# Last-value rows loaded before the first keys, and value differences formed from the fifth pair on with three buffers

## The chip, the cores and the metric

The kernel runs on one core of a Trainium2 chip. A core has five engines with queues of their own: TensorE (PE in the profile, with PEld for its weight loads), VectorE (DVE), ScalarE (ACT), GpSimd (POOL) and SyncE (SP). In this kernel SP issues nearly all DMAs; its queue is in order, and so is each other engine's. The metric is the device time of one execution in microseconds, lower is better.

## The reference

One step of a hybrid encoder layer, for a prompt of 1024 tokens and 64 new tokens of a running stream with 512 cached ones. Cut to what matters:

```python
def project(x, norm_w, w_in, q_norm_w, k_norm_w):
    h = rms_norm(x, norm_w) @ w_in                      # 1024 -> 6144 columns
    sb_q, sb_k, sb_v, sb_z, cb_q, cb_k, cb_v, cb_z, g_sb, g_cb = jnp.split(h, SPLIT_POINTS, axis=-1)
    ...                                                 # cb_q and cb_k are normalized per head

def stick_breaking(q, k, v, q_pos, k_pos):
    z = jnp.einsum("bqhd,bkhd->bhqk", q, k).astype(jnp.float32) * ATTN_SCALE
    causal = k_pos[None, :] < q_pos[:, None]
    log_beta = jax.nn.log_sigmoid(z)
    log_keep = jnp.where(causal, jax.nn.log_sigmoid(-z), 0.0)
    suffix = lax.cumsum(log_keep, axis=3, reverse=True) - log_keep
    w = jnp.where(causal, jnp.exp(log_beta + suffix), 0.0)
    return jnp.einsum("bhqk,bkhd->bqhd", w.astype(v.dtype), v)

def merge(x, o_sb, z_sb, o_cb, z_cb, g_sb, g_cb, w_proj_sb, w_proj_cb, w_out):
    b_sb = (o_sb * jax.nn.silu(z_sb)) @ w_proj_sb
    b_cb = (o_cb * jax.nn.silu(z_cb)) @ w_proj_cb
    h = jax.nn.sigmoid(g_sb) * b_sb + jax.nn.sigmoid(g_cb) * b_cb
    return x + h @ w_out
```

The second branch (cb) is a softmax attention over a band of nine chunks of 64 keys. There are eight heads of 64 in each branch. Projected keys and values are also outputs.

## The kernel before

**Stages.** The first stage (to 226 us) normalizes and transposes x and forms the projections whose tokens stay on the partitions: the values of both branches and the queries and keys of cb. The second stage (226 to 531 us) forms the rest of the input projection in 14 *pairs* of 128-column units: pairs 1 to 4 are keys and queries of sb, 5 to 8 the gates z, 9 to 12 the sigmoid of the sb gate, 13 and 14 part of the cb gate. Each pair runs seven steps `s` of 2 x 12 matmuls (L672), one product of a fast 2 x 2 scheme, so there are 98 steps, counted by `n`. The third stage is attention: stick-breaking (sb) over 4 pairs of heads and then the band (cb), with the four last projection units as fill work between (L832). Then come the merge and the output projection.

**Differences of values.** The stick-breaking weights of a query row are differences of a running product, so the kernel multiplies the running products with differences of values instead: row t of `d_dv` in DRAM is value row t-1 minus value row t, and the last value of each query tile is added afterwards (`vl`, L1181). The 26 jobs of 128 rows (L628 to L634) are spread over the second stage. `dv_load` (L610) loads two tiles, `dva` with the rows shifted by one (L614 where there is no row before the first: 127 rows, the first being zeroed by POOL; L618 else) and `dvb` with the rows themselves (L620). `dv_sub` (L623) subtracts on POOL (L625) and puts the store to `d_dv` (L626) on the list that `step()` empties at the next step. `dv_step` loads at odd n and subtracts at even n, as soon as two jobs are loaded. Both tiles have two buffers.

**Around it.** Each pair's results go through `emit` (L567): ACT writes them into an `hl` tile (L574 for gates, L580 for keys and queries; four buffers), DVE completes it (L576, L581), and the store to DRAM (L571, L51) is issued by SP at the next step. Weights of the next pairs are loaded by SP too (L391), split by ACT, DVE and POOL (L435, L436, L403). All of these stand in the order in which the code is written; there is no scheduler.

**Between the stages.** After the pairs, SP loads what the first scores need: keys of the cache and of the new tokens (`kss`), queries of the new tokens (`sqs`), keys (`ks`) and queries of the prompt (`sq`, of which three tiles cover query tiles 0 to 2, 3 to 5 and 6, 7), then the differences (`vp`, `vs`) and the gate (`zt`). Between these loads stand six calls of `fill(24)`, each of which gives PE 24 fill matmuls, and the stores of their results (`d_gcb<-sg`, L745). `load_vl` (L723) loads the last value row of every query tile, 8 + 1 rows, into `vrow`; `make_vl` (L727) transposes them on PE after the six fills and before the first scores (L1080). The scans of `imp` and `ims` (L715, L719) on DVE prepare two masks in the same pool of buffers as `vrow`.

**DMA slots.** SP's DMAs count on eight semaphores in turn (DMAHW0 to DMAHW7), and a DMA waits until the one eight places before it has landed. An engine that takes over memory of the earlier stage waits for all the eight.

Of the kernel before, what the change touches and what calls it, by code (L numbers as in the profile page):

```python
# [8 lines left out]
F32 = mybir.dt.float32  # L9
# [23 lines left out]
def hybrid_step_kernel(ctx: ExitStack, tc: tile.TileContext, x_prompt, x_sample, c_sbk, c_sbv, c_cbk, c_cbv,  # L33
# [26 lines left out]
    def xc(t):  # L60

        return t * 128 if t < 4 else HF + (t - 4) * 128
# [69 lines left out]
    def load_unit(j):  # L132
        c = units[j][1]
        W.load(("u", j), wpool, w_in[:, c:c + 128].rearrange("(k p) n -> p k n", p=128), [128, KT, 128])
# [7 lines left out]
    def xk(s, k):  # L142
        return xhl[s][k // 4][:, k % 4]
# [56 lines left out]
    with ExitStack() as ph:  # L200
# [192 lines left out]
        def presum(n):  # L393

            i, s = divmod(n, 7)
            if i >= len(pairs) or s not in (1, 4, 6):
                return
            a, b = slice(0, 128), slice(128, 256)
            r1, r2 = raws[2 * i], raws[2 * i + 1]

            def total(x, y, op):
                d = ws.tile([128, 4, 128], F32, name="ws")
                V.tensor_tensor(out=d, in0=x, in1=y, op=op)  # L403
                return d[:]

            if s == 1:
                sums[1] = total(r1[:, :, b], r2[:, :, b], OP.add)
                sums[2] = total(sums[1], r1[:, :, a], OP.subtract)
            elif s == 4:
                sums[3] = total(r1[:, :, a], r1[:, :, b], OP.subtract)  # L410
                load_raw(2 * i + 3)
            else:
                sums[4] = total(r2[:, :, a], sums[2], OP.subtract)

        def prep(n):

            i, s = divmod(n, 7)
            if i >= len(pairs):
                return
            a, b = slice(0, 128), slice(128, 256)  # L420
            r1, r2 = raws[2 * i], raws[2 * i + 1] if s else None
            if s == 0:
                src = r1[:, :, a]
            elif s == 3:
                src = r2[:, :, a]
            elif s == 5:
                src = r2[:, :, b]
            else:
                src = sums[{1: 2, 2: 1, 4: 3, 6: 4}[s]]
            shape = [128, 2, 4, 128]  # L430
            if s in (2, 3, 4):
                t = natx.tile(shape, F32R, name="wlox" if s == 3 else "whix", bufs=2)
            else:
                t = wpool.tile(shape, F32R, name="whi" if s in (0, 5) else "wlo", bufs=2)
            A.activation(t[:, 0], src, AF.Copy)  # L435
            G.tensor_tensor(out=t[:, 1], in0=src, in1=t[:, 0].bitcast(F32), op=OP.subtract)  # L436
            blk[n] = t
            if s == 6:
                load_raw(2 * i + 4)
# [12 lines left out]
        for i in range(nb):  # L452
            for ti, t in enumerate(TO):
# [7 lines left out]
                for m, (k, n) in enumerate(steps):  # L461
# [3 lines left out]
                    x = xs[:, k] if t == 8 else xk(n % 2, k)[:, xc(t):xc(t) + r]  # L465
# [80 lines left out]
    with ExitStack() as ph:  # L546
        up = ph.enter_context(tc.tile_pool(name="a2u", bufs=3, side="right"))
# [7 lines left out]
        def step():  # L555
            for e in later[:]:
                e[0] -= 1
                if e[0] < 0:
                    later.remove(e)
                    e[1]()  # L560
# [47 lines left out]
        dvs = []  # L608

        def dv_load(r0, rows_, cur, prev, c):  # L610
            a, b = (up.tile([128, 256], F32, name=x, bufs=2) for x in ("dva", "dvb"))
            if len(prev) == 1 and prev[0] is None:
                G.memset(a[0:1], 0.0)
                SP.dma_start(a[1:rows_], cur[0:rows_ - 1, c])  # L614
            else:
                o = 0
                for q in prev:
                    SP.dma_start(a[o:o + q.shape[0]], q[:, c])  # L618
                    o += q.shape[0]
            SP.dma_start(b[:rows_], cur[:, c])  # L620
            dvs.append((r0, rows_, c, a, b))
# [29 lines left out]
        for i in range(len(pairs)):  # L651
            bank, s1, u2, u3 = {}, {}, {}, {}
            for s in range(7):
                n = 7 * i + s
                prep(n + LEAD)
                presum(n + LEAD + 1)
                if n + LEAD == 7 * len(pairs) + 2:
                    W.split(("u", 0))
                if n + LEAD == 7 * len(pairs) + 1:
                    load_unit(1)  # L660
                step()
                if i > 1:
                    dv_step(n % 2)
                w = blk.pop(n)
                for c, (a, b) in enumerate(XC):
                    m = b - a
                    if s < 3:
                        bank[BANK[s], c] = psB.tile([128, 512], F32, name=f"b{BANK[s]}{c}")
                    ps = bank[BANK[s], c]
                    for k in range(4):  # L670
                        for e, (hl_, x) in enumerate(((0, 0), (0, 1), (1, 0))):
                            TE.matmul(ps[:, :m], w[:, hl_, k], right[s](x)[:, k, a:b], start=s < 3 and k == 0 and e == 0,  # L672
                                      stop=k == 3 and e == 2, skip_group_check=s > 2)
                    if s == 0:
                        s1[c] = up.tile([128, 288], F32, name="s1")
                        A.activation(s1[c][:, :m], ps[:, :m], AF.Copy)
                    elif s in (1, 4):
                        u = up.tile([128, 288], F32, name="u2" if s == 1 else "u3")
                        (u2 if s == 1 else u3)[c] = u
                        V.tensor_tensor(out=u[:, :m], in0=ps[:, :m], in1=s1[c][:, :m], op=OP.add)  # L680
                    elif s == 3:
                        emit(i, 0, 0, c, ps, True)
                    elif s == 5:
                        V.tensor_tensor(out=s1[c][:, :m], in0=ps[:, :m], in1=s1[c][:, :m], op=OP.add)  # L684
                        emit(i, 1, 0, c, s1[c], False)
                    elif s == 6:
                        V.tensor_tensor(out=u2[c][:, :m], in0=ps[:, :m], in1=u2[c][:, :m], op=OP.add)
                        emit(i, 0, 1, c, u2[c], False)
                if s == 4:
                    for c, (a, b) in enumerate(XC):  # L690
                        m = b - a
                        V.tensor_tensor(out=u3[c][:, :m], in0=bank["3", c][:, :m], in1=u3[c][:, :m], op=OP.add)
                        emit(i, 1, 1, c, u3[c], False)
# [29 lines left out]
    def load_vl():  # L723
        SP.dma_start(vrow[0:8], d_sbv[0:NP].rearrange("(t q) c -> t q c", q=128)[:, 127])
        SP.dma_start(vrow[8:9], d_sbv[T - 1:T])
# [54 lines left out]
    def load_v(b, p):  # L780
        src, cache, n0 = (d_dv, d_dv[NP:NP + PAST], NP + PAST) if b == "sb" else (d_cbv, c_cbv, NP)
        c = slice(p * 128, (p + 1) * 128)
        vp = am.tile([128, 8, 128], F32, name="vp", bufs=2)
        vs = am.tile([128, 5, 128], F32, name="vs", bufs=1)
        SP.dma_start(vp, src[0:NP, c].rearrange("(t q) c -> q t c", q=128))
        SP.dma_start(vs[:, 0:4], cache[:, c].rearrange("(t q) c -> q t c", q=128))
        SP.dma_start(vs[0:64, 4], src[n0:n0 + NS, c])
        VP[b, p] = (vp, vs)
# [7 lines left out]
    def load_k(b, p, s):  # L796
        if s:
            place_k(alloc_k((b, p), 1), d_cT[b][p][:], 0, 512, 0, 512)
            place_k(KS[(b, p), 1], d_kT[b][p][:], NP, T, 512, 576)
        else:  # L800
            place_k(alloc_k((b, p), 0), d_kT[b][p][:], 0, NP, 0, NP)
# [345 lines left out]
    def load_z(b, p, j):  # L1147
        zt = am.tile([128, 256], F32, name="zt", bufs=4)
        nq = 256 if j < 4 else 64
        SP.dma_start(zt[:, :nq], d_z[b][p][:, 256 * j:256 * j + nq])  # L1150
        zts[b, p, j] = zt
# [59 lines left out]
    def load_bias(h):  # L1211
# [6 lines left out]
        if h % 2:  # L1218
            bs = BI["s", h // 2] = ab.tile([128, 576], F32, name="bsm", bufs=1)
            for w in range(2):  # L1220
                src = d_rb[h - 1 + w][0:1, 127:128]
                SP.dma_start(bs[64 * w:64 * w + 64], bass.AP(tensor=src.tensor, offset=src.offset,
                                                             ap=[[767, 64], [1, 576]]))

    load_k("sb", 0, 1)
    for f in (lambda: load_q("sb", 0, 3), lambda: load_k("sb", 0, 0), lambda: load_q("sb", 0, 0),
              lambda: (load_v("sb", 0), load_z("sb", 0, 4)), load_vl, lambda: None):
        fill(24)
        flush()
        f()  # L1230
# [10 lines left out]
    for i in range(len(seq) + LAG + 1):  # L1241
        m = 0
        if i < len(seq):
            b, p, t, hd = seq[i]
# [30 lines left out]
        if 0 <= i - LAG < len(seq):  # L1275
            tr(i - LAG)
            b, p, t, hd = seq[i - LAG]
# [182 lines left out]
    for i in range(2):  # L1460
# [3 lines left out]
        for q, s in enumerate(OP_):  # L1464
# [14 lines left out]
            for c in range(2) if s != "b" else ():  # L1479
# [25 lines left out]
                if s in (3, 4, 5, 6):  # L1505
# [3 lines left out]
                    x = {3: xrs.pop((i, w, half, c)) if s == 3 else None, 4: None, 5: s1[c], 6: u2[c]}[s]  # L1509
                    if s == 4:  # L1510
                        p, x = u3[c], xrs.pop((i, 1, 1, c))
# [61 lines left out]
```

## Time and profile before

| what | us |
|---|---|
| runs shown | 1003.59, 1005.52, 1006.38; median 1005.52 |
| profiled execution | 1004.52, its span 1002.7 |
| PE busy | 964.6, granted clock 0.993 on the mean |
| second stage (14 pairs) | 226 to 531 |
| fills before attention | 531 to 554.8 |
| first transposes of `vrow` | 560.31 |

All times in rows are counted from the span's start. A row of waits reads "engine line <- what ended the wait: total us, times, longest us"; one of a timeline "start us, length us, engine line operation out<-in xcount", with the idle time ahead of it and what ended that in brackets. SPq and ACTq are the engines' own queues, where DMAs are issued and semaphores awaited.

### The profile page before, as it was taken

Reading aid. Unit: us, or ns where it says so; the run is one execution under the profiler, and the core shown is the slowest. Engines: PE = TensorE matmul, PEld = TensorE weight load, DVE = VectorE, ACT = ScalarE, POOL = GpSimd, SP = SyncE. Lnnn points to the kernel's source line nnn. Section 1 sums busy time; section 2 is a strip of 40 time slices with the busy share of each in tenths; the row PEclk is TensorE's granted clock in tenths of the full one; section 3 lists DMA queues with packets and bytes.
Section 4 is the critical chain, followed back from the end, with each engine's and each line's share of the span. In section 5 each row is a group of like instructions: output and inputs, shape, how many; then the busy total and the mean of one; then the engine's idle time right before and its main releaser. Section 6 shows DMA issues by size and latency. Waiting matters only on the chain.

```text
span 1002.7 us, 20526 instructions
## 1 busy us (share of the span) xinstructions
PE 964.6 (96%) x7620; PEld 918.0 (92%) x7620; DVE 592.6 (59%) x1168; ACT 479.5 (48%) x1056; POOL 360.8 (36%) x325
## 2 busy tenths in 40 slices
PE   5999999999999899999999799999999899999998
PEld 5999999999999899999999688877978787999998
DVE  5456673894454465533222369776667666499745
ACT  5544443444443333334332367666877776465320
POOL 3276663205454566565430000000210100386551
PEclk9999999999999999999999799999999999999999
DMA  7636577434667455464325887679697771863642
GB/s 241 218 102 212 187 248 267 138 98 155 186 190 226 151 166 154 148 189 132 92 73 163 230 197 195 153 198 240 194 253 212 225 216 36 250 198 99 200 131 88
DMA packets 182984, 176.81 MB, mean 176 GB/s; under 512 B 35873, under 2 KB 168733, under 8 KB 182758
## 3 DMA queue, kind: packets, MB, share of 16 engines
q1 hardware_dynamic: 174166, 167.19, 56.3%
q10 hardware_dynamic: 8720, 8.33, 2.6%
q8 instruction: 60, 0.98, 0.4%
q14 instruction: 38, 0.31, 0.1%
HBM read 113.46 MB, written 62.00 MB: 175 GB/s over the span
## 4 chain that ended last, share of the span: by engine, by line
PE 80%; DMA 9%; SPq 3%; ACT 3%; DVE 2%; issue 2%; POOL 1%; ACTq 0%; DVEq 0%; POOLq 0%
PE b L672 23%; PE acc L466 19%; PE b L1487 8%; PE o L1172 7%; PE z L1080 6%; PE pt L1133 6%; PE b L974 5%; PE acc L932 3%; PE acc L832 2%; DMA d_dv<-dva 2%; DMA zt<-d_zcb 1%; SPq L51 1%; DMA gt<-d_gsb 1%; DMA d_zsb<-hl 1%; PE pk L351 1%
## 5 line engine op out<-in xcount | busy, mean ns | idle before, releaser
L1133 PE MATMUL pt<-ident,be 128*128 128x128 f32 (+1 forms) x568 | 88.5, 280 | 6.0 <-ACT wT L1142 2.4
L1080 PE MATMUL z<-ks,sq 128*128 128x320 f32 (+5 forms) x384 | 86.9, 335 | 4.1 <-DVE sm L1085 3.8
L1102 DVE TENSOR_TENSOR_SCAN be<-be,imp 128x128 f32<-128x128 f32 (+7 forms) x64 | 83.6, 1342 | 4.8 <-ACT be L1083 4.7
L1133 PEld LDWEIGHTS pt<-ident,be 128*128 128x128 f32 (+1 forms) x568 | 65.8, 141 | 19.0 <-issue 5.8
L1142 ACT ACTIVATE wT<-pt 128x512 f32<-128x512 f32 (+3 forms) x125 | 57.1, 485 | 49.6 <-PE pt L1133 48.4
L466 PE MATMUL acc<-whi,xa 128*128 128x256 f32 x256 | 74.2, 292 | 0.0
L1215 POOL MEMSET bias<- 64x64 f32 x8 | 1.2, 144 | 200.8 <-DMA bias<-d_rb 188.3
L1080 PEld LDWEIGHTS z<-ks,sq 128*128 128x128 f32 x384 | 66.3, 193 | 6.0 <-DVE sm L1085 4.5
L123 POOL TENSOR_TENSOR wlo<-wraw,whi 128x1024 fp32r<-128x1024 f32 x15 | 36.8, 2456 | 97.1 <-ACT whi L116 70.7
L466 PE MATMUL acc<-wlox,xm 128*128 128x256 f32 x256 | 70.7, 278 | 0.0
L466 PE MATMUL acc<-whi,xm 128*128 128x256 f32 x256 | 70.7, 278 | 0.0
L466 PE MATMUL acc<-wlo,xa 128*128 128x256 f32 x256 | 70.7, 278 | 0.0
L466 PE MATMUL acc<-whix,xb 128*128 128x256 f32 x256 | 70.6, 278 | 0.0
L466 PE MATMUL acc<-whix,xm 128*128 128x256 f32 x256 | 70.6, 278 | 0.0
L680 DVE TENSOR_TENSOR u<-b,s 128x256 f32<-128x256 f32 (+1 forms) x56 | 23.9, 439 | 73.5 <-PE b L672 58.4
L1172 PE MATMUL o<-wT,vp 128*64 128x256 f32 (+1 forms) x608 | 67.2, 357 | 0.1
L1172 PEld LDWEIGHTS o<-wT,vp 128*64 128x64 f32 x608 | 44.3, 136 | 23.1 <-issue 5.2
L1105 ACT ACTIVATE be<-be,sm 128x640 f32<-128x640 f32 (+5 forms) x68 | 47.2, 694 | 15.8 <-DVE sm L1104 15.5
L1083 ACT ACTIVATE be<-z 128x384 f32<-128x384 f32 (+6 forms) x104 | 47.4, 493 | 9.9 <-PE z L1080 9.5
L436 POOL TENSOR_TENSOR whix<-ws,whix 128x512 fp32r<-128x512 f32 x28 | 36.9, 1317 | 39.5 <-ACT whix L435 39.5
L1093 ACT ACTIVATE be<-be,sm 128x640 f32<-128x640 f32 (+5 forms) x68 | 47.2, 695 | 3.2 <-DVE sm L1085 2.7
L672 PE MATMUL b<-t1h,wlo 128*128 128x256 f32 (+1 forms) x224 | 45.5, 292 | 2.8 <-DVE s L684 2.8
(303 smaller groups left out, 3179.9 us busy)
## 6 DMA issues: line engine op xcount, KB each, us to landing
wraw<-in_w_in_dram SPq DMA_DIRECT2D x31, 512.0 KB, 5.2
wrawx<-in_w_in_dram SPq DMA_DIRECT2D x17, 512.0 KB, 4.1
sq<-d_qsbT SPq DMA_DIRECT2D x32, 192.0 KB, 4.2
sq<-d_qcbT SPq DMA_DIRECT2D x32, 192.0 KB, 5.0
xt<-in_x_prompt_dram SPq DMA_DIRECT2D x8, 512.0 KB, 3.5
d_kcbT<-hl SPq DMA_DIRECT2D x8, 512.0 KB
d_qcbT<-hl SPq DMA_DIRECT2D x8, 512.0 KB, 5.6
d_ksbT<-hl SPq DMA_DIRECT2D x16, 256.0 KB, 2.6
```

What stands on the lines that cost most here:

```text
L466: TE.matmul(ps, x, w, start=m == 0, stop=m == len(steps) - 1)
L672: TE.matmul(ps[:, :m], w[:, hl_, k], right[s](x)[:, k, a:b], start=s < 3 and k == 0 and e == 0, stop=k == 3 and e == 2, skip_group_check=s ...
L974: TE.matmul(pp[uu][:, :n], w[:, p, uu * 128:uu * 128 + 128], g[:, a:e], start=p == 0 and m == 0, stop=p == NPAIR - 1 and m == 2)
L1080: TE.matmul(z[:, :m], s[:, e, q0:q0 + 128], ks[:, h, o + x:o + y], start=e == parts[0][0], stop=e == parts[-1][0])
L1083: A.activation(be[:r, x:y], z[:r, :m], AF.Sigmoid, scale=-0.125)
L1093: A.activation(be[:, :n], be[:, :n], AF.Exp, bias=kp[:, j:j + 1], scale=-1.0, accum_out=kp[:, 2:3])
L1102: V.tensor_tensor_scan(be[:r, n - 1::-1], be[:r, n - 1::-1], im[:, ::-1], 0.0, op0=OP.mult, op1=OP.max)
L1105: A.activation(be[:r, :n], be[:r, :n], AF.Copy, scale=kp[:r, 3:4])
L1133: TE.transpose(pt[:kr, x, :r], be[:r, kb * 128:kb * 128 + kr], ident[:r, :r])
L1142: A.activation(w[:, sl:sl + m, q0:q0 + r], pt[:, :m, :r], AF.Copy)
L1172: TE.matmul(o[hd * 64:hd * 64 + 64, c0:c1], vv[:kr, kb, hd * 64:hd * 64 + 64], wT[b, p, j, hd, s // 4][:kr, s % 4, c0:c1] if j < 4 else wT ...
L1487: TE.matmul(ps[:, t], left[s](xs_, k)[:, ts_], wt_[:, k], start=s < 3 and t == k == e == 0, stop=k == 3 and e == 2, skip_group_check=s > 2 ...
```

## The change

Three edits: `dva` and `dvb` get three buffers each instead of two; the steps that load and subtract begin with the fifth pair instead of the third (`i > 3`); and the two loads of `vrow` are issued first of all after the pairs, ahead of `kss`, where they stood after the fifth fill before.

```diff
         def dv_load(r0, rows_, cur, prev, c):
-            a, b = (up.tile([128, 256], F32, name=x, bufs=2) for x in ("dva", "dvb"))
+            a, b = (up.tile([128, 256], F32, name=x, bufs=3) for x in ("dva", "dvb"))
...
                 step()
-                if i > 1:
+                if i > 3:
                     dv_step(n % 2)
...
+    load_vl()
     load_k("sb", 0, 1)
     for f in (lambda: load_q("sb", 0, 3), lambda: load_k("sb", 0, 0), lambda: load_q("sb", 0, 0),
-              lambda: (load_v("sb", 0), load_z("sb", 0, 4)), load_vl, lambda: None):
+              lambda: (load_v("sb", 0), load_z("sb", 0, 4)), lambda: None, lambda: None):
         fill(24)
         flush()
         f()
     make_vl()
```

SP's queue at the start of the fifth pair (`d_zsb` is where the gates z go; minus is before, plus is after):

```order
-L626 DMA d_dv<-dva 128x256
-L618 DMA dva<-d_sbv 128x256
-L620 DMA dvb<-d_sbv 128x256
-L626 DMA d_dv<-dva 128x256
-L614 DMA dva<-in_cache_sb_v_dram 127x256
-L620 DMA dvb<-in_cache_sb_v_dram 128x256
+L614 DMA dva<-d_sbv 127x256
+L620 DMA dvb<-d_sbv 128x256
+L618 DMA dva<-d_sbv 128x256
+L620 DMA dvb<-d_sbv 128x256
 L571 DMA d_zsb_86<-hl 128x256 x2
 L571 DMA d_zsb_86<-hl 128x32
```

Before, the eighth and ninth jobs stand here, each load behind a store of differences; now the first two jobs do, and no store is ahead of them.

SP's queue at the end of the pairs, with the semaphores that each row waits for (a piece of the changed kernel; before, `d_gcb_104` is followed by `kss` at once, which waits for one slot at a time):

```order
L571 DMA d_gcb_104<-hl 128x32 [waits DMAHW6_49]
L724 DMA vrow<-d_sbv 8x512 [waits DMAHW4_49,DMAHW3_49,DMAHW5_49,DMAHW2_49,DMAHW6_49,DMAHW1_49,DMAHW7_49,DMAHW0_49,DVE_49]
L725 DMA vrow<-d_sbv 1x512
L51 DMA kss<-d_csbT_78 64x512 [waits PE_49]
L51 DMA kss<-d_csbT_78 64x512 x3
```

The first `vrow` load now waits for all eight slots; the `kss` loads behind it no longer wait for any.

DVE's queue at the same place, alike in both kernels:

```order
L687 TENSOR_TENSOR u_6975<-b_6992,u_6975 128x256 [waits PE_49]
L687 TENSOR_TENSOR u_6990<-b_7005,u_6990 128x288 [waits PE_49]
L715 SCALAR_TENSOR_TENSOR imp<-ident 128x128 [waits DMAHW4_49,DMAHW3_49,DMAHW5_49,DMAHW2_49,DMAHW6_49,DMAHW1_49,DMAHW7_49,DMAHW0_49,Activation_49]
L719 SCALAR_TENSOR_TENSOR ims<-ident 64x64 x2
L123 TENSOR_TENSOR wlo<-wraw,whi 128x1024 [waits Activation_49,Pool_49]
```

The scan L715 has the same eight slots to wait for as the `vrow` load in its new place.

## The prediction

> **What bounds the kernel now.** I read the page first: TensorE (PE) is busy almost throughout.
>
> ```profile
> span 1002.7 us, 20526 instructions
> PE 964.6 (96%) x7620; PEld 918.0 (92%) x7620; DVE 592.6 (59%) x1168; ACT 479.5 (48%) x1056; POOL 360.8 (36%) x325
> PE 80%; DMA 9%; SPq 3%; ACT 3%; DVE 2%; issue 2%; POOL 1%; ACTq 0%; DVEq 0%; POOLq 0%
> ```
>
> So the change can pay only where PE stands still or runs slowly, and it issues the same instructions as before. The second view is PE's waits in the two stretches that the diff touches: the 14 pairs of projection units (226 to 531 us; first three rows) and the start of attention (526 to 620; last row). Columns: total us, times, longest.
>
> ```profile
> PE b L672 <- DVE s L684: 2.8, 1, 2.8
> PE b L672 <- ACT s L676: 0.7, 1, 0.7
> PE b L672 <- DVE u L687: 0.3, 1, 0.3
> ...
> PE pt L730 <- DMA d_gcb<-sg: 5.5, 1, 5.5
> ```
>
> The third view is the table by stretches, cut where PE stops (columns: length, busy time of PE, PEld, DVE, ACT, POOL, then the granted clock, DMA share, GB/s).
>
> ```profile
> 344.97:348.38 3.41, 3.41 (x15) 3.41 (x16) 2.09 (x5) 1.77 (x5) 2.17 (x2) 0.50 0.46 145
> 450.00:531.00 81.00, 81.00 (x654) 81.00 (x653) 24.92 (x51) 29.51 (x65) 33.51 (x25) 1.00 0.35 105
> 554.80:560.00 5.20, 0.04 (x1) 0.00 (x0) 0.00 (x0) 0.44 (x1) 0.00 (x0) 1.00 1.01 254
> 560.01:570.25 10.24, 9.59 (x53) 8.71 (x54) 3.71 (x8) 3.76 (x11) 0.00 (x0) 0.50 0.90 234
> ```
>
> Each long stop is followed by a stretch at half clock: 3.41 us after the stop of 2.8, 10.24 us after the stop of 5.5. The differences are formed by these subtractions on GpSimd (POOL), the last of which starts at 446.9; from 450 us on PE has no gap at all for 81 us.
>
> ```profile
> L625 POOL TENSOR_TENSOR dva<-dva,dvb x26: 729/745/1247, 288.9 to 446.9; 128x256 f32<-128x256 f32 x24, 64x256 f32<-64x256 f32 x2
> ```
>
> **The first stop, in the pairs.** SyncE's (SP's) waits from 270 to 450 us:
>
> ```profile
> SPq L618 <- DMA d_dv<-dva: 40.6, 16, 6.2
> SPq L614 <- DMA d_dv<-dva: 5.3, 3, 2.6
> ```
>
> And the chain of work from 326 to 350 us (start, length, what):
>
> ```profile
> 327.19 4.25 DMA d_dv<-dva
> 331.45 0.32 SPq L618
> 332.35 2.10 DMA d_dv<-dva
> 334.46 0.26 SPq L614
> 335.35 8.12 DMA d_zsb<-hl
> 343.55 0.42 ACT hl L574
> 344.85 5.18 PE b L672 x27
> ```
>
> With two buffers the load for the third job needs the buffer whose result is still being stored, and that store was issued just ahead of it. SP therefore stands for 45.9 us in all, 2.4 us on average and 6.2 at most, with everything behind it in its queue late. ScalarE's (ACT's) rows show what that does:
>
> ```profile
> 329.78 0.69 ACT L574 ACTIVATE hl<-b 128x256 f32<-128x256 f32 x2
> 343.55 0.42 ACT L574 ACTIVATE hl<-s 128x256 f32<-128x256 f32 x1 [9.17 <-DMA d_zsb<-hl]
> ```
>
> The values of 329.78 were stored only from 335.35, 5 us late, behind a load of 127 rows (L614); they landed 8.12 us later; ACT needed that `hl` buffer again, VectorE (DVE) waited for ACT, PE for DVE.
>
> **The second stop, before attention.** SP, DVE and PE, in that order:
>
> ```profile
> 533.04 2.39 SPq L51 DMA_DIRECT2D kss<-d_csbT  x4
> 556.45 0.33 SPq L724 DMA_DIRECT2D vrow<-d_sbv  x1
> 557.23 0.23 SPq L725 DMA_DIRECT2D vrow<-d_sbv  x1
> 557.55 0.82 SPq L745 DMA_DIRECT2D d_gcb<-sg  x2
> 564.17 0.59 SPq L1150 DMA_DIRECT2D zt<-d_zsb  x1
> 534.27 0.42 DVE L715 TENSOR_TENSOR_SCAN imp<-ident 128x128 f32<-128x128 f32 x1 [2.67 <-DMA d_gcb<-hl]
> 563.63 1.36 DVE L1102 TENSOR_TENSOR_SCAN be<-be,ims 128x576 f32<-128x576 f32 x1 [2.52 <-ACT be L1083]
> 573.16 0.61 DVE L1181 SCALAR_TENSOR_TENSOR zt<-o,vl,zt 128x128 f32<-128x128 f32 x2
> 554.53 0.30 PE L832 MATMUL acc<-xm,wlo 128*128 128x320 f32 x1
> 560.31 0.56 PE L730 MATMUL pt<-ident,vrow 9*128 9x9 f32 x4 [5.48 <-DMA d_gcb<-sg]
> 571.52 0.63 PE L1080 MATMUL z<-ks,sq 128*128 128x512 f32 x2
> ```
>
> PE has done its fill matmuls at 554.84 and the next thing in its order are the transposes of `vrow`, whose loads SP issues only at 556.45 and 557.23. The profile names a store that ended at the same time; by the program the transposes wait for the rows.
>
> **The change part by part.**
>
> *Third buffer, and differences from the fifth pair on.* The 26 subtractions and all their DMAs stay; they move 14 steps later (steps 29 to 82 of 98), so pairs 3 and 4 lose them and pairs 10 to 12 gain them. A load now waits for a store issued two steps earlier. A step is 24 matmuls, about 3 us (PE's stretch of 81 us holds 654 matmuls, 0.124 us each), so the store has 6 us, against the 6.2 us of the longest SP wait and an average of 45.9 / 19 = 2.4. The wait goes almost wholly. What is late next: the four 127-row loads, which remain, but with SP on time their neighbours are issued some 5 us earlier than at 335.35, and the lateness that reached PE was 2.8. Gain: 2.8 + 0.7 + 0.3 = 3.8 us of waits and 3.41 x 0.5 = 1.7 us of half clock, 5.5 at most. I take 5.0, leaving 0.5 for a small wait such as the 0.7 above. The ends: 1.0 if one load stops PE again as at 344.85 (2.8 + 1.7 = 4.5 back), 5.5 if none does. The work moved into pairs 10 to 12 costs POOL 0.745 us per subtraction on an engine that is busy 33.51 of 81 us there, and SP's queue; both are covered by PE's matmuls as in pairs 5 to 10 before. Two more KB per partition cost nothing that the order shows.
>
> *Rows of last values first.* The transposes find `vrow` in place, so PE goes on at 554.84 instead of 560.31: 5.5 us. Half clock then need not come. From 560.31 to the score matmuls at 571.52 (the fourth query tile's second head) lie 11.2 us, 9.9 of them at half clock. With all of that bound by PE, full clock would save 5; with none, nothing. Part is bound by the chain sigmoid, scan (1.36), transposes. I take 3: PE would be ready for them at about 563 instead of 571.5.
>
> Against this stands SP. In its new place the first `vrow` load waits for all eight DMA slots, that is, for every store then under way. DVE's scan `imp` waits for the same eight and starts at 534.27, so I price the wait by it: 534.27 - 533.04 = 1.2 us, plus 0.7 for the two issues (0.33 + 0.23 and the gaps). All later loads are 1.9 us late until SP passes the old place, where it saves 557.55 - 556.45 = 1.1. The bounds of this price are 0.7 (no wait) and 0.7 + 4.25, the slowest store row above. The keys and queries of the first tiles had landed with room; the next ones are what is late:
>
> ```profile
> L51 SPq DMA_DIRECT2D sq<-d_qsbT x8: 524/601/602, 559.1 to 563.5; - x8
> sq<-d_qsbT SPq DMA_DIRECT2D x4, 192.0 KB, 3.5
> ```
>
> The fourth of these eight (0.64 us apart) is issued at 561.0, after the change at 561.8, and lands 3.5 later at 565.3. So the matmuls of 571.52 start at 565.3 and not at 563: 6.2 us earlier. The gate `zt` comes at 564.17 + 0.8 + 3.5 = 568.5; DVE used it at 573.16: 4.7 us earlier. Between 4.7 and 6.2 I take 5.5. From there on attention is PE's work (80% of the chain), so the gain is carried to the end. Ends: 2 (both DMA delays worse by the upper price, or the clock drops again) and 5.5 + 5 = 10.5 (no tile late).
>
> [...]
>
> Sum: 5.0 + 5.5 = 10.5 us off the profiled execution's 1004.52 gives 994.0. The median of the runs shown is 1005.52, 1.0 more; I put half of that on top: 994.5.
>
> **Rivals.**
> - *A: the first stop comes back.* One of the 127-row loads, now at the corresponding step of a later pair, stops PE as at 344.85. Gain 1.0 + 5.5: 998.5. For it: this load comes in the fourth step of a pair again, just ahead of the stores. Against it: SP is no longer late there.
> - *B: tiles late and clock down in attention.* PE stops for the queries instead, about 2.3 us (565.3 - 563), near the 2.8 that halved the clock. Two windows of 3.41 at half cost 3.4: 998.
> - *C: no change.* A and B together, or the third buffer still waiting: gain 2, 1003.
> - *D: slower.* All four 127-row loads stop PE. They start at these times:
>
> ```profile
> L614 SPq DMA_DIRECT2D dva<-d_sbv x2: 250/326/401, 278.3 to 367.2; - x2
> L614 SPq DMA_DIRECT2D dva<-in_cache_sb_v_dram x2: 255/255/255, 334.5 to 417.4; - x2
> ```
>
> Only the one of 334.5 precedes a long stop. Were all four to do so, 4 x 4.5 = 18 against 5.5 before is 12.5 lost, less 5.5 gained: 1011.5. It decides from the third stop on (3 x 4.5 = 13.5 against 5.5 + 5.5 = 11.0). [...]
> - *E: better than I think*, no tile late: 989.
>
> **Chances.** Main case 0.55 (991 to 997), A 0.15, B 0.13, C 0.06, D 0.08, E 0.03. Some 0.3% (3 us) is what a measurement tells from no change. Faster: main, A, B, E = 0.86; same: C = 0.06; slower: D = 0.08. The range from 989 to 1001.5 takes in the main case, A and B with 3 us of spread above them, and E's near end; it leaves out C and D.
>
> **What would show it.** Right: no PE wait over 1 us between 226 and 530 us and no half clock there; SP's waits for `d_dv` under 10 us; the `vrow` load issued about 1.2 us after the last `d_gcb<-hl` store; no stop at the transposes L730, a stop of 1 to 3 us at the fourth query tile; no or one half-clock window near it. Wrong: a stop with half clock in pairs 5 to 12 behind a 127-row load (A, D); half clock in attention's first 15 us (B); or a gain at 570 us that a later stop in attention takes back, which nothing here prices.

## The result, and the profile after

The changed kernel takes 993.88 us (median of 992.19 to 994.92) against 1004.56 us of the kernel before beside it: a ratio of 0.9897, 95% interval 0.9864 to 0.9929. Two more sets of runs of the same kernel gave 0.9913 (0.9893 to 0.9932) and 0.9912 (0.9883 to 0.9940), so the gain is 8.7 to 10.3 us by the medians. The forecast, 994.5 us, is 0.989 of the median that was shown (1005.52).

The page of the changed kernel:

```profile
span 993.1 us, 20513 instructions
PE 963.3 (97%) x7620; PEld 918.2 (92%) x7620; DVE 595.4 (60%) x1168; ACT 479.3 (48%) x1056; POOL 355.7 (36%) x325
PE 89%; DMA 4%; SPq 2%; DVE 2%; ACT 2%; issue 1%; POOL 0%; DVEq 0%; ACTq 0%
```

PE is busy as long as before (963.3 us, 964.6 before) in a span that is 9.6 us shorter. DMA's share of the chain falls from 9% to 4%.

PE's waits (engine line <- what ended it: total us, times, longest). From 224 to 527 us the view has no row at all; at the start of attention, 526 to 620 us, its largest two are:

```profile
PE z L1080 <- DMA sq<-d_qsbT: 3.5, 2, 3.1
PE pt L1133 <- DVE be L1102: 0.9, 1, 0.9
```

The stop at the transposes of `vrow` (L730, 5.5 us) is gone; a stop for the queries of tiles 3 to 5 stands there now.

SP's waits from 270 to 520 us; of those for a store of differences one is left, 1.1 us against 45.9:

```profile
SPq L571 <- ACT hl L574: 25.9, 12, 7.5
SPq L618 <- DMA d_dv<-dva: 1.1, 1, 1.1
```

The table by stretches (length, busy time of PE, PEld, DVE, ACT, POOL, granted clock, DMA share, GB/s) has full clock through the whole second stage, one half-clock window after the stop for the queries, and two later ones that the profile of before does not have:

```profile
224.00:526.00 302.00, 302.00 (x2421) 301.14 (x2420) 138.94 (x266) 116.19 (x265) 158.16 (x128) 1.00 0.52 157
561.99:565.40 3.41, 3.41 (x16) 2.15 (x15) 0.82 (x1) 1.04 (x2) 0.00 (x0) 0.50 1.01 247
684.87:688.28 3.41, 3.11 (x14) 2.64 (x16) 0.84 (x5) 3.36 (x10) 0.00 (x0) 0.50 0.82 224
780.45:783.86 3.41, 3.41 (x14) 3.31 (x14) 3.21 (x13) 3.21 (x5) 0.00 (x0) 0.50 0.58 166
```

The timeline around the transition, SP, then DVE, then PE:

```profile
529.21 0.28 SPq L724 DMA_DIRECT2D vrow<-d_sbv  x1
529.84 2.38 SPq L51 DMA_DIRECT2D kss<-d_csbT  x4
554.80 5.50 SPq L51 DMA_DIRECT2D sq<-d_qsbT  x8
529.10 0.42 DVE L715 TENSOR_TENSOR_SCAN imp<-ident 128x128 f32<-128x128 f32 x1 [2.66 <-DMA d_gcb<-hl]
565.46 0.61 DVE L1181 SCALAR_TENSOR_TENSOR zt<-o,vl,zt 128x128 f32<-128x128 f32 x2 [2.65 <-DMA zt<-d_zsb]
549.45 0.30 PE L832 MATMUL acc<-xm,wlo 128*128 128x320 f32 x1
549.68 0.41 PE L730 MATMUL pt<-ident,vrow 9*128 9x9 f32 x4
560.19 0.73 PE L1080 MATMUL z<-ks,sq 128*128 128x512 f32 x2 [3.13 <-DMA sq<-d_qsbT]
561.69 0.92 PE L1080 MATMUL z<-ks,sq 128*128 128x512 f32 x2 [0.37 <-DMA sq<-d_qsbT]
```

Set beside the rows of before, the gain can be read in steps. The last fill matmul starts at 549.45 against 554.53: 5.1 us come from the second stage. The second head of the fourth query tile starts at 561.69 against 571.52: 9.8 us, so 4.7 more come from the transition. The span is 9.6 us shorter. These are single executions: in two later profiles of the change the last fill starts at 546.80 and 547.00, 2.5 us sooner again, with no wait of PE in the pairs in any of the three.

### The profile page after: what moved, and what is told of

It reads as the page before. It is cut to its first block, busy times and chain, and to the rows that moved or that the text cites. A ratio compares the mean times of both kernels' runs of the same rounds, so it can differ in the third digit from the quotient of the medians.

```text
span 993.1 us, 20513 instructions
## 1 busy us (share of the span) xinstructions
PE 963.3 (97%) x7620; PEld 918.2 (92%) x7620; DVE 595.4 (60%) x1168; ACT 479.3 (48%) x1056; POOL 355.7 (36%) x325
## 4 chain that ended last, share of the span: by engine, by line
PE 89%; DMA 4%; SPq 2%; DVE 2%; ACT 2%; issue 1%; POOL 0%; DVEq 0%; ACTq 0%
PE b L672 30%; PE acc L466 19%; PE b L1488 8%; PE o L1172 7%; PE pt L1133 6%; PE z L1080 6%; PE b L974 5%; PE acc L932 3%; PE acc L832 2%; SPq L51 1%; DMA wrawx<-in_w_in_dram 1%; PE pk L351 1%; DMA zt<-d_zcb 1%; DMA gt<-d_gsb 1%; PE pt L279 1%
## 5 line engine op out<-in xcount | busy, mean ns | idle before, releaser
L1105 ACT ACTIVATE be<-be,sm 128x640 f32<-128x640 f32 (+5 forms) x68 | 47.2, 694 | 13.3 <-DVE sm L1104 13.0
L466 PEld LDWEIGHTS acc<-whi,xa 128*128 128x128 f32 x256 | 47.9, 188 | 0.1
```

The costliest lines, as they stand in the source:

```text
L466: TE.matmul(ps, x, w, start=m == 0, stop=m == len(steps) - 1)
L1105: A.activation(be[:r, :n], be[:r, :n], AF.Copy, scale=kp[:r, 3:4])
```

## The experiments

Each kernel was timed in five rounds beside the kernel before, on one chip with the others of its set. A gain in us is the ratio's distance from 1 times the median of before in that set (1000.82 us for the first four, 1002.66 for the next four, 1002.52 for the last four). Profiles are of one execution each.

### The first stop: which half of the edit, and what cause

**Rows of last values first, alone** (the kernel before with one edit):

```diff
+    load_vl()
     load_k("sb", 0, 1)
...
-              lambda: (load_v("sb", 0), load_z("sb", 0, 4)), load_vl, lambda: None):
+              lambda: (load_v("sb", 0), load_z("sb", 0, 4)), lambda: None, lambda: None):
```

> Only the vrow loads are moved to the front; the differences stay as before. If the two parts are independent, as the prediction summed them: the stop of 5.5 us at the transposes L730 and its 10.24 us of half clock go, a stop of 2 to 3 us for the queries of the fourth query tile comes in their place, the stop of 2.8 us in the pairs stays; 5.5 us less than before (4.7 to 6.2), about 999. Rival, the late loads only move the stop (half clock comes back with it): less than 3 us gained.

Measured: 997.23 us, ratio 0.9971 (0.9954 to 0.9987), a gain of 2.9 us (1.3 to 4.6). PE's waits in the second stage and at the start of attention:

```profile
PE b L672 <- DVE s L684: 2.4, 1, 2.4
PE z L1080 <- DMA sq<-d_qsbT: 2.4, 1, 2.4
```

The stop in the pairs stays, the one at L730 goes, and one for the queries comes, with a half-clock window of 3.41 us behind it (from 562.27). The places are as expected; the gain is about half of what the forecast gave this edit (5.5), and is what the rival named (half clock comes back, less than 3 us).

**Differences later, with three buffers, alone:**

```diff
-            a, b = (up.tile([128, 256], F32, name=x, bufs=2) for x in ("dva", "dvb"))
+            a, b = (up.tile([128, 256], F32, name=x, bufs=3) for x in ("dva", "dvb"))
...
-                if i > 1:
+                if i > 3:
```

> Only the differences are changed (from the fifth pair, three buffers); vrow is loaded where it was. Independent parts: no PE wait over 1 us in the pairs and no half clock there, the stop at L730 stays at about 5.5 us with its half clock; 5.0 us less than before, about 999.5. Rival, the gain in the pairs depends on what follows: under 3 us.

Measured: 995.32 us, ratio 0.9955 (0.9937 to 0.9972), a gain of 4.5 us (2.8 to 6.3). There is no PE wait in the pairs; the stop at L730 stays, in this execution with 6.9 us:

```profile
PE pt L730 <- DMA d_gcb<-sg: 6.9, 1, 6.9
```

The two halves together give 7.4 us by these medians, against 8.7 to 10.3 for the whole change: they add up within the intervals.

**Three buffers alone** (`bufs=3`, still from the third pair on) and **two buffers, later** (`i > 3` alone):

> Third buffer alone, differences still from the third pair. If SP's wait for the buffer is the cause of the first stop: SP's waits of L618 and L614 for d_dv fall from 45.9 us to under 10, the stop of 2.8 us goes and its half clock with it, 5 us less than before. Rival, the load of 127 rows is the cause: it still stands ahead of the gate stores of the fifth pair, the stop stays, 0 to 1 us gained.

> Differences from the fifth pair on, but two buffers. If SP's wait for the buffer is the cause: SP's waits for d_dv stay near 46 us and a stop of 1 to 3 us with half clock shows up in pairs 5 to 12; 0 to 2 us gained. Rival, it is the place that matters (the keys' and queries' stores of pairs 3 and 4 made SP late): no stop, 4 to 5.5 us gained.

Measured: 997.06 us, ratio 0.9959 (0.9943 to 0.9976), a gain of 4.1 us, with three buffers; 994.31 us, ratio 0.9952 (0.9930 to 0.9973), a gain of 4.8 us, with the later start. Either edit removes the whole first stop. With three buffers no wait of SP for a store of differences is left, as expected. The second is a miss: SP still waits for the stores as long as before, yet PE does not stop. SP's waits in the kernel with two buffers and the later start:

```profile
SPq L618 <- DMA d_dv<-dva: 41.7, 17, 5.4
SPq L614 <- DMA d_dv<-dva: 6.4, 3, 3.3
```

So the sum of SP's waits is not what decides. The trace shows what differs at the place of the stop: the first matmul of the pair in which the second 127-row load stands, and the `d_zsb` stores behind that load, in the kernel before (fifth pair) and with the later start (seventh pair):

```profile
315.46 0.28 PE L672 MATMUL b<-xa,whi 128*128 128x256 f32 x1
335.35 3.14 SPq L571 DMA_DIRECT2D d_zsb<-hl  x3
```

```profile
357.36 0.28 PE L672 MATMUL b<-xa,whi 128*128 128x256 f32 x1
373.42 1.74 SPq L571 DMA_DIRECT2D d_zsb<-hl  x3
```

Before, the store is issued 19.9 us into its pair; with the later start 16.1, and with three buffers 14.4 (331.14 - 316.74). SP's own part is not what the later start changes: from ACT's write of these values to the issue of their store it is 5.6 us in both (335.35 - 329.78 and 373.42 - 367.86), against 2.7 with three buffers. What changes is the write, 14.3 us into the fifth pair and 10.5 into the seventh. In the fifth pair ACT comes late, having waited for a store of queries and loaded a table; in the seventh no table is loaded, and the wait at that place is 2.26 us. The two rows of the fifth pair:

```profile
322.00 0.42 ACT L580 ACTIVATE hl<-u 128x256 fp32r<-128x256 f32 x1 [3.89 <-DMA d_qsbT<-hl]
328.48 1.28 ACT L574 ACT_TABLE_LOAD   x1
```

So the place matters, as the rival of the later start's expectation said, but by way of ACT. What share the wait and the table load have in it is not shown.

**The 127-row loads split** (the kernel before; each of them becomes a load of 112 rows and one of 15):

```diff
-                SP.dma_start(a[1:rows_], cur[0:rows_ - 1, c])
+                SP.dma_start(a[1:113], cur[0:112, c])
+                SP.dma_start(a[113:rows_], cur[112:rows_ - 1, c])
```

> The kernel before, but each load of 127 rows is made as two, of 112 and 15 rows; two buffers, differences from the third pair as before. Theory now (from the lag of that load in the runs so far: 9.0 and 9.5 us with a stop, 2.8 to 5.1 without): the stop of 2.8 us needs both SP's lateness and the 8 us landing of the 127 rows. Then the landing falls to about 2 to 3 us, SP's waits for d_dv stay near 46 us, the stop and its half clock go, about 4.5 us less. Rival, SP's lateness alone is enough: the stop stays over 1.5 us, 0 to 1 us less.

Measured: 998.14 us, ratio 0.9957 (0.9942 to 0.9971), a gain of 4.3 us. SP's waits and PE's waits in the pairs, then the DMAs issued from 335.2 to 336.8 us (KB each, us to landing):

```profile
SPq L619 <- DMA d_dv<-dva: 33.1, 17, 3.5
SPq L614 <- DMA d_dv<-dva: 6.1, 3, 3.4
PE b L673 <- DVE u L688: 0.4, 1, 0.4
PE b L673 <- DVE u L681: 0.3, 1, 0.3
```

```profile
d_zsb<-hl SPq DMA_DIRECT2D x2, 128.0 KB, 2.2
```

The `d_zsb` store that took 8.12 us behind a load of 127 rows takes about 2.2 us behind the split one, although SP is as late there as before: the store is issued 20.7 us into its pair (335.83 - 315.17), and SP's waits sum to 39.2 us against 45.9. From 335.2 to 336.8 us the DMA engines moved 0.20 MB with the split (126 GB/s) and 0.14 before (86 GB/s). What in the load of 127 rows holds the store up is not shown.

**One scale for all of these.** ScalarE's row for the first `s` value behind the second 127-row load, which stands in the fourth step of its pair in all of them, shows how long ACT waits there for the `d_zsb` store (the idle time in brackets). In the change, with the rows alone, with three buffers, with the later start, with the split, and in a kernel with dull matmuls before attention that is told of below, in that order:

```profile
377.64 0.42 ACT L574 ACTIVATE hl<-s 128x256 f32<-128x256 f32 x1 [1.68 <-DMA d_zsb<-hl]
```

```profile
341.86 0.42 ACT L574 ACTIVATE hl<-s 128x256 f32<-128x256 f32 x1 [8.31 <-DMA d_zsb<-hl]
```

```profile
340.01 0.42 ACT L574 ACTIVATE hl<-s 128x256 f32<-128x256 f32 x1 [5.03 <-DMA d_zsb<-hl]
```

```profile
379.86 0.42 ACT L574 ACTIVATE hl<-s 128x256 f32<-128x256 f32 x1 [4.35 <-DMA d_zsb<-hl]
```

```profile
338.03 0.42 ACT L574 ACTIVATE hl<-s 128x256 f32<-128x256 f32 x1 [3.86 <-DMA d_zsb<-hl]
```

```profile
342.81 0.42 ACT L574 ACTIVATE hl<-s 128x256 f32<-128x256 f32 x1 [8.17 <-DMA d_zsb<-hl]
PE b L672 <- DVE s L684: 1.8, 1, 1.8
```

| kernel | ACT waits for the store, us | PE's stop there, us |
|---|---|---|
| before | 9.17 | 2.8 |
| rows alone | 8.31 | 2.4 |
| before with dull matmuls | 8.17 | 1.8 |
| three buffers | 5.03 | none |
| later start, two buffers | 4.35 | none |
| split loads | 3.86 | none |
| the change | 1.68 (2.98 and 2.75 in its two later profiles) | none |

Between ACT's wait and PE's stop lie about 6 us of slack (9.17 - 2.8 = 6.4, 8.31 - 2.4 = 5.9, 8.17 - 1.8 = 6.4). What exceeds it reaches PE. Each of the three cures takes 4 to 5 us off a wait that was some 3 us too long, and so each alone is enough: three buffers and the later start together gained 4.5 us, as each does alone, and the split added to a variant of the change (in the last set, below) brings nothing more that the runs can tell (0.9922 against 0.9923).

### The second stop: half clock, late tiles, and what is carried to the end

**PE kept busy through the stop** (the kernel before; nobody reads what these matmuls produce):

```diff
+    dull = psF.tile([128, 512], F32, name="acc")
+    for x in range(30):
+        TE.matmul(dull[:, :384], xk(0, 0)[:, 0:128], xk(0, x % 4)[:, 0:384], start=x == 0, stop=x == 29)
     make_vl()
```

> The kernel before with 30 more matmuls of 384 columns (0.16 us each, 4.8 us in all) ahead of the transposes L730, whose results nobody reads: PE works through the stop of 5.5 us, and the rows still come when they come. This measures the half clock by itself. Theory: no half clock after 555 us, the scores of the fourth query tile about 3 us nearer to the transposes than the 11.2 us of before, 3 us less in all. Rival, that stretch is bound by sigmoid, scan and DMA: within 1 us of before.

Measured: 1001.75 us, ratio 0.9995 (0.9978 to 1.0011): between 2.2 us less and 1.1 more. The table shows the clock kept up where before it was 0.50, and the timeline PE's two rows that matter:

```profile
560.00:570.24 10.24, 8.48 (x72) 7.02 (x71) 6.14 (x10) 5.71 (x16) 0.00 (x0) 1.00 0.88 207
```

```profile
560.71 0.38 PE L730 MATMUL pt<-ident,vrow 9*128 9x9 f32 x4 [0.64 <-DMA d_gcb<-sg]
568.73 0.63 PE L1080 MATMUL z<-ks,sq 128*128 128x512 f32 x2
```

The 30 dull matmuls take 5.37 us in this trace, 0.18 each, where 0.16 was expected. In this execution the fourth query tile's second head comes at 568.73, 2.8 us sooner than before's 571.52, though L730 is 0.4 us later. So at that place, in these two executions, full clock is worth about what the forecast took (3 us). In the runs little of it is left at the end, 0.5 us by the ratio, and 3 us lies outside the interval: the expectation missed, and its rival (within 1 us) fits.

**The change again, and the change with another order of loads.** In the second, `vs`, the gate and the second query tile are loaded ahead of the weights of the fills and `vp` after them:

```diff
-        SP.dma_start(vp, src[0:NP, c].rearrange("(t q) c -> q t c", q=128))
+        if (b, p) != ("sb", 0):
+            SP.dma_start(vp, src[0:NP, c].rearrange("(t q) c -> q t c", q=128))
...
+    def load_vp():
+        SP.dma_start(VP["sb", 0][0], d_dv[0:NP, 0:128].rearrange("(t q) c -> q t c", q=128))
...
-              lambda: (load_v("sb", 0), load_z("sb", 0, 4)), lambda: None, lambda: None):
+              lambda: (load_v("sb", 0), load_z("sb", 0, 4), load_q("sb", 0, 1)), load_vp, lambda: None):
```

> The changed kernel itself once more, beside the single edits. If the parts add up: rows first alone gave a ratio of 0.9971 and the differences alone 0.9955, so 0.993 is expected. If each part uncovers the other's gain (the first predicted sum, 10.5 us): 0.990.

> The changed kernel, with the query tile of query tiles 3 to 5 loaded right after vs and zt and ahead of vp and the weights, which come later. Theory: the stop of 3.1 us at the fourth query tile goes and the half clock near 562 with it, 3 to 5 us less than the changed kernel (3.1 + 1.7 = 4.8 at most). Rival, DMA throughput is full there and another tile (vp for the first full query tiles, or zt) takes its place: under 1.5 us.

Measured: 993.40 us, ratio 0.9913 (0.9893 to 0.9932), for the change; 992.54 us, ratio 0.9902 (0.9882 to 0.9923), with the other order: 0.9 us between the medians, less than the runs can tell. Both values expected of the change, 0.990 and 0.993, lie in its interval, so the runs do not tell whether the two parts add or help each other. Of the other order 3 to 5 us were expected and are not seen; as its rival said, the stop for the queries goes, and another tile, now the late one, stops PE:

```profile
558.42 0.87 PE L1176 MATMUL o<-wT,vp 128*64 128x256 f32 x8 [2.17 <-DMA vp<-d_dv]
```

**The rows of last values inside the pairs.** The last set starts from the change. In its first kernel the rows are loaded at step 86 and transposed at step 92, so that nothing waits for all eight DMA slots ahead of `kss`; the second adds the other order of loads; the third adds the split of the 127-row loads; the fourth is the change again.

```diff
+                if n == 86:
+                    load_vl()
+                if n == 92:
+                    make_vl()
...
-    load_vl()
     load_k("sb", 0, 1)
...
-    make_vl()
```

> The changed kernel with the rows of last values loaded and transposed inside the last pair (at steps 86 and 92 of 98), so that no load of `vrow` stands ahead of `kss` and no DMA waits there for all eight slots. My theory (SP's lateness sets when the fourth query tile lands): `kss` is issued 1.9 us earlier, `sq` 1.9 us earlier, the stop of 3.1 to 3.4 us for it shrinks to 1.2 to 1.5 us and its half clock goes: 1 to 2 us below the changed kernel of this batch. Rival (the tiles land when the DMA engines have moved what is ahead of them, however early they are issued): `sq` is issued earlier but lands later after its issue, the stop stays above 2.5 us, and the time is the changed kernel's within 0.5 us.

> The former with `vs`, `zt` and the second query tile loaded ahead of the weights, and `vp` after them. Where SP's lateness is the cause, the 2.2 us stop for `vp` that this order had alone shrinks under 0.5 us and no stop above 1 us is left before 600 us: 1.5 to 3 us below the changed kernel of this batch. Rival (bound by what the DMA engines move): a stop of about 2 us stays, at `vp`, and the time is as with the order alone, about 1 us below the changed kernel.

> The former with each 127-row load split into 112 and 15 rows. No stop is left in the pairs, so my theory expects nothing: within 0.7 us of the former. Rival (slow landings cost PE something in the pairs even where no stop above 0.3 us shows): 1 to 3 us less.

> The changed kernel again, as a reference on this chip: 0.99 of the kernel before, 992 to 995 us, with a stop of about 3 us for the fourth query tile.

Measured, in that order: 994.35 us (ratio 0.9923, 0.9897 to 0.9950), 994.93 us (0.9923, 0.9895 to 0.9951), 994.09 us (0.9922, 0.9894 to 0.9950), and the change 994.28 us (0.9912, 0.9883 to 0.9940). None of the three is seen to beat the change, where 1 to 3 us were expected of the first two; the intervals are some 2.8 us to each side, so that a gain of 1 us or so is not excluded. The third lies 0.8 us below the second, where at most 0.7 was expected; the runs cannot tell that from nothing. The stops for a late tile, in the first, the third and the change:

```profile
558.49 0.73 PE L1084 MATMUL z<-ks,sq 128*128 128x512 f32 x2 [2.58 <-DMA sq<-d_qsbT]
```

```profile
PE o L1181 <- DMA vp<-d_dv: 2.4, 1, 2.4
```

```profile
558.12 0.73 PE L1080 MATMUL z<-ks,sq 128*128 128x512 f32 x2 [3.31 <-DMA sq<-d_qsbT]
```

Taking the eight-slot wait away shortened the stop from 3.3 to 2.6 us, not to 1.2 to 1.5. Counted from the last fill, the stop ends 1.5 us sooner (558.49 - 548.85 against 558.12 - 547.00), but PE, without the transposes, comes to it sooner too, and that takes back part. The queries take 4.7 us to land in both, so the rival's later landing is not seen. In the second kernel the stop for `vp` is 1.6 us where under 0.5 was expected; no half-clock window follows it.

The time from the last fill matmul's start to the first sixteen products `o<-wT,vp` measures the whole transition, in one execution of each kernel. In this table it stands beside the ratio to the kernel before, since the medians of different sets cannot be compared:

| kernel | last fill, us | sixteen products, us | between | ratio |
|---|---|---|---|---|
| before | 554.53 | 578.18 | 23.7 | 1 |
| differences alone | 547.49 | 572.41 | 24.9 | 0.9955 |
| before, dull matmuls | 554.55 | 575.39 | 20.8 | 0.9995 |
| rows alone | 551.84 | 571.03 | 19.2 | 0.9971 |
| change | 549.45 | 569.78 | 20.3 | 0.9897 |
| change, second set | 546.80 | 568.49 | 21.7 | 0.9913 |
| change, third set | 547.00 | 567.38 | 20.4 | 0.9912 |
| change, other order of loads | 547.33 | 565.91 | 18.6 | 0.9902 |
| rows in the pairs | 548.85 | 568.24 | 19.4 | 0.9923 |
| rows in the pairs, other order | 549.96 | 566.04 | 16.1 | 0.9923 |

The first two rows have the same transition in the program and differ by 1.2 us, and so do the three of the change, by up to 1.4. The last kernel has the shortest transition, by 4.3 us against the change of its set, and no better time. PE's largest waits from 570 to 850 us in it, and in the change of the same set:

```profile
PE z L1088 <- DVE sm L1093: 3.7, 2, 3.4
PE pt L1141 <- ACT be L1113: 3.5, 3, 2.9
PE pt L1141 <- ACT wT L1150: 2.4, 3, 1.8
```

```profile
PE pt L1133 <- ACT be L1105: 2.1, 3, 1.5
PE pt L1133 <- DVE sm L1085: 1.8, 1, 1.8
```

All rows of that view sum to 13.3 us in the first and to 8.2 in the second: the later stops, behind VectorE and ScalarE, cost 5.1 us more where PE came 4.3 us sooner. Such stops also differ between executions of the change alone (at the `sm` wait of L1085 past 720 us its first profile has 1.8 us, that of this set none), so it stays open whether they come from PE's arriving sooner or by chance. Chance is likely to have a large part: the execution profiled of the first kernel took 997.91 us, 3.0 above its median, that of the change 989.95, 4.3 below its own, and the first has two half-clock windows past 620 us (from 682.99 and 781.98) where the second has none. The runs of the last kernel and of the dull matmuls still point to gains of the transition that are not all found at the end.

## Why the prediction was right, and where it was not

The result, 993.88 us, is 0.6 us from the forecast of 994.5, and the main case happened. Step by step:

- *Third buffer and later start, 5.0 us.* The profile has 5.1 at the last fill (its two later ones 7.5 and 7.7) and the runs of this edit alone 4.5 (2.8 to 6.3). SP's waits fell to 1.1 us (under 10 was named), the clock is full in the pairs, and no 127-row load stops PE, so rivals A and D did not come. The cause was only half told. The forecast put the stop on SP's waits; with these left in place, a later start or a split load removes it just as well. It takes both, a store issued late in its pair (after 18.6 to 20.5 us in the three kernels that stop, 14.4 and 16.1 with three buffers and the later start) and a load of 127 rows just ahead of it, to push ACT's wait past 6 us of slack.
- *SP 1.9 us late behind the eight-slot wait.* Before's `kss` at 533.04 less the 5.1 us gained is 527.9; it came at 529.84, 1.9 late. The price read from DVE's scan was exact.
- *No stop at L730, then PE waiting for the fourth query tile.* Both came, with one window of half clock. The stop was 3.1 us, above the 1 to 3 named: the queries took 4.7 us to land and not the 3.5 of the row of before. So the scores are 4.7 us earlier by the transition and not 6.2; the gate `zt`, used at 565.46 after 573.16, is 7.7 - 5.1 = 2.6 us earlier and not 4.7. The forecast held landing times constant, and the same loads took 3.5 us in one place and 4.7 in another; why is not shown. Part of rival B was in this: one half-clock window after that stop stands in the forecast's list of what would show it right, and half clock in attention's first 15 us in its list for B, so this sign does not tell the two apart; the times do (998 for B).
- *5.5 us for the second edit.* This is the term that was too large: 2.9 us (1.3 to 4.6) in the runs of that edit alone. The step that failed is the sizing inside the transition: the stop for the queries was longer and the gate came only 2.6 us sooner, and up to the sixteen products the transition is 2.0 to 4.5 us shorter than before's in the three profiles of the change and the one of the rows alone. About that much is found in the runs, so for this edit "the gain is carried to the end" is not refuted. As a rule it is not safe: the dull matmuls gained 2.8 us at the fourth query tile and 0.5 at the end, and the shortest transition brought nothing that the runs can tell. The share of the chain, from which the forecast took it, is an average.
- *The sum.* A first term sized rightly (5.0) and a second one sized too high (5.5) give 10.5, against a total that the three sets of runs put at 8.7 to 10.3 us. The halves alone sum to 7.4 us, and their intervals do not exclude that the rest comes from the two together. That the forecast is off by 0.6 us only is luck in part: the set with the result has the largest gain of the three.

## What to carry to other kernels

Follow a stop upstream to the wait that has the most slack, and measure that slack: here ACT's wait could grow by 6 us unseen, and any of three small edits that brought it under that was worth the stop with its half clock, 4 to 5 us, once. When a stop at the start of a stage is removed, look for the next tile in the queue that will be late, and count what is saved there only as far as runs show it at the end of the stage. A load of 127 rows is worth splitting into 112 and 15 where a store behind it makes the engine that bounds the kernel wait, as it did here; where that stop was gone already, the split brought nothing that the runs can tell.

## What the runs showed of the hardware

- The load of 127 rows delayed the store issued behind it: the `d_zsb` store landed after 8.12 us, and after 2.2 us when the load was split. In the change, where the load stays whole, a `d_zsb` store of 16 KB behind it (issued at 372.04) still took 6.13 us; there it stops nobody.
- The clock fell to 0.50 for 3.41 us after stops shorter than 2.8 us too: after 2.4 us in the pairs with the rows alone (from 343.82), and after 1.8 us in the kernel with dull matmuls (the row below). In the change's first profile a later stop of 1.8 us is also followed by such a window (at 684.87); in its other two profiles the stop at that place is as long and the clock stays up (1.00 from 684 to 688), as it does in before after a stop of 2.5 us (ended at 790.16; 1.00 from there to 795). So in these runs the length of one stop does not decide; what else does is not shown.

```profile
344.52:347.93 3.41, 3.41 (x17) 3.41 (x17) 2.37 (x5) 1.77 (x5) 2.17 (x2) 0.50 0.28 69
```

- A stretch of 10.24 us at half clock, replaced by one at full clock with dull matmuls, changed the time by 0.5 us (between 2.2 less and 1.1 more).
